# Context rows of a two-layer diffusion block: normalised rows written to memory and transposed behind four token tiles

## The chip, the cores and the metric

The kernel runs on one core of one Trainium2 chip. The metric is the device time of one execution in microseconds, the median of several runs. Each run is one launch of the whole program.

## The reference

Two layers work on 1024 latent tokens and 256 context tokens of width 1024. Layer 0 is grouped-query attention, layer 1 multi-head latent attention. Both begin in the same way, and layer 1 reads what layer 0 has made:

```python
h  = rms_norm(x, norm_w)   * (1.0 + scale[:, None, :]) + shift[:, None, :]
hc = rms_norm(ctx, norm_w) * (1.0 + scale_c) + shift_c
...
k, kr = split(h @ w_in ...)          # layer 1: 256 latent columns and 32 rotary columns
kv = rms_norm(kv_a, kv_a_norm) @ w_kv_b
k_nope, v = split(kv); k_rope = axial_rope(rms_norm(k_r, k_rope_norm))
...
x   = x + gate * y
ctx = ctx + gate_c * yc              # layer 0 only
```

Layer 1 needs the context for its keys and values alone, and only the latent stream is returned.

## The kernel before

Everything is float32. A product of two matrices is made of three products of TensorE (PE), of the high and low parts of both operands (`mm3`, lines 93 to 95); a high part is a cast on ScalarE (ACT), a low part a subtraction on VectorE (DVE) or, in turn, on GpSimd (POOL) (`sub_any`, line 136). Tokens come in ten tiles of 128 rows: tiles 0 to 7 are latent, 8 and 9 the context. DMAs are issued by SP, in the order of its queue; an issue that has to wait holds up those behind it.

Around the change the program has two stages.

The first is the output projection of layer 0 (`out_proj`, from line 710). For each tile in turn PE makes two products of 512 columns (`y`), DVE multiplies them by the gate (line 750), DVE and POOL add the residual (line 751), and `sink0` follows. `sink0` writes a latent tile to `x1d` in memory (line 1363), normalises its rows in place in the tile `xt` (`norm_rows`: the squares on ACT, line 256, their root on POOL, line 119, the scaling on DVE, line 258) and collects pairs of tiles. `flush` calls `modulate` for a pair, one tile later than it is complete: PE transposes the two tiles' rows in 16 pieces (line 270), DVE applies layer 1's scale and shift (line 274), ACT casts (line 278), and DVE or POOL subtracts. The result is `hh`, `hl`: the operand of layer 1's products, with tokens as columns. The last pair is the context; its `flush` stands behind the loop.

The second stage makes layer 1's keys and values. `staged` runs five steps over the ten tiles, each step some tiles behind the one before: `kv_compress` (24 products of 288 columns, then squares, roots and scaling to the row tile `kvn`, lines 1431 to 1440, and for the 32 rotary columns four small steps on POOL, lines 1447 to 1450), `kv_latent` (transposes of `kvn` by PE, lines 1457 and 1458, and their split `kvh`, `kvl`), `kv_expand` (24 products of 512 columns into `mmk` and `mmv`, the keys scaled by line 1470) and `kv_store` (line 1506 on). The products of `out_proj`, `kv_compress` and `kv_expand` share four PSUM buffers (`ps_mm`). At the beginning of this stage SP loads `w_kv_b` in four pieces of 512 KB, two pieces of the next weight, and small tables (line 1396: `bc_l1_kv_a_norm` and others; line 1401: `ropeB`). These tables lie in memory that the first stage's row tiles held. Three `wraw` buffers take the raw weights, so a piece is loaded only when an earlier one has been split.

A scheduler orders the instructions of both stages, but DVE keeps the order of the program text in the second.

Of the kernel before, what the change touches and what calls it, by code (L numbers as in the profile page):

```python
# [10 lines left out]
F32 = mybir.dt.float32  # L11
# [8 lines left out]
P = 128  # L20
D = 1024
KT = D // P
NL = 1024
NC = 256
NT = NL + NC
TL = NL // P
# [10 lines left out]
def hybrid_kernel(ctx: ExitStack, tc: tile.TileContext, ins: dict, out: bass.AP):  # L37
    nc = tc.nc
    pe, act, dve, pool, sp = nc.tensor, nc.scalar, nc.vector, nc.gpsimd, nc.sync
# [24 lines left out]
    x1d = dram.tile([NT, D], F32, name="x1d")  # L64
# [188 lines left out]
    def norm_rows(xt, small):  # L253
        junk = small.tile([P, D], BF16, name="junk", tag="junk", bufs=1)
        ss = small.tile([P, 1], F32, name="xss", tag="xss")
        act.activation(junk, xt, AF.Square, accum_out=ss)
        rs = rstd_of(small, ss, D, "x")
        dve.tensor_scalar(xt, xt, rs, None, op0=ALU.mult)

    def modulate(l, pair, xs, hT, ps_tp, tmpp, share=2, k2s=range(KT // 2)):  # L260

        cond = 1 if pair == 4 else 0
        hh, hl = hT[cond]
        cs = slice(0, 256) if cond else slice(pair * 256, pair * 256 + 256)
        for k2 in k2s:
            t = ps_tp.tile([P, 512], F32, name="tp", tag="tp")
            for kk in range(2):
                for j in range(2):
                    k = 2 * k2 + kk
                    pe.transpose(t[:, kk * 256 + j * P: kk * 256 + (j + 1) * P], xs[j][:, k * P:(k + 1) * P], ident)  # L270
            h = tmpp.tile([P, 512], F32, name="hmod", tag="w512")
            for kk in range(2):
                k = 2 * k2 + kk
                dve.tensor_scalar(h[:, kk * 256:(kk + 1) * 256], t[:, kk * 256:(kk + 1) * 256],
                                  A[l][:, k, cond:cond + 1], Bv[l][:, k, cond:cond + 1], op0=ALU.mult, op1=ALU.add)
            hv = h.rearrange("p (k n) -> p k n", k=2)
            hi = hh[:, 2 * k2:2 * k2 + 2, cs]
            act.copy(hi, hv)
            sub_any(hl[:, 2 * k2:2 * k2 + 2, cs], hv, raw(hi), share)
# [29 lines left out]
    class Attention:  # L309
# [382 lines left out]
        def flush(self):  # L692
            self.run_deferred(1 << 30)
# [94 lines left out]
    ps_tp = stT.enter_context(tc.tile_pool(name="pstp0", bufs=3, space=PSUM, reuse_waits="tile"))  # L788
# [554 lines left out]
    with ExitStack() as st:  # L1343
        xp = st.enter_context(tc.tile_pool(name="xpp0", bufs=4, **right))
        gp = st.enter_context(tc.tile_pool(name="gp0", bufs=1, **right))
        wk = st.enter_context(tc.tile_pool(name="wk1a", bufs=3, **right))
        small = st.enter_context(tc.tile_pool(name="sml1a", bufs=3, **right))
        pad(small, 224)
        stO = ExitStack()
        op = stO.enter_context(tc.tile_pool(name="opp0", bufs=3, **right))  # L1350
        hold = []
        hT1 = []

        def flush(upto):
            while len(hold) >= upto and hold:
                pair, xs = hold.pop(0)
                modulate(1, pair, xs, hT1, ps_tp, wk)

        xs_of = {}

        def sink0(tt, xt):
            if tt < TL:
                sp.dma_start(x1d[tt * P:(tt + 1) * P, :], xt)
            norm_rows(xt, small)
            xs_of.setdefault(tt // 2, []).append(xt)
            if tt % 2 == 0:
                flush(1)
            else:
                hold.append((tt // 2, xs_of[tt // 2]))

        def started0():
            at.flush()
            stL.close()
            hT1.append(alloc_hT(stl, "hlat1", NL))

        def resid0(tt):
            return x_in[tt * P:(tt + 1) * P, :] if tt < TL else ctx_in[(tt - TL) * P:(tt - TL + 1) * P, :]

        out_proj(0, wo, resid0, sink0, TT, op, xp, gp, ps_mm, first, started0, False)
        stO.close()  # L1380
        hT1.append(alloc_hT(stc, "hctx1", NC))
        flush(1)
    hT = hT1


# [2 lines left out]
    def proj1(tt, w, cols):  # L1388
        ps = ps_mm.tile([P, 512], F32, name="mm", tag="mm")
        lh, ll = h_cols(hT, tt)  # L1390
        mm3(ps[:, :cols], lh, ll, lambda k: w[0][:, k, :], lambda k: w[1][:, k, :], range(KT))
        return ps

    def bcast(tab, name, n):
        t = tab.tile([P, n], F32, name="bc_" + name)
        sp.dma_start(t, ins[name].rearrange("(o d) -> o d", o=1).broadcast_to([P, n]))
        return t
# [12 lines left out]
    with ExitStack() as st:  # L1410
# [4 lines left out]
        latp = st.enter_context(tc.tile_pool(name="latp1a", bufs=4, **right))  # L1415
        small = st.enter_context(tc.tile_pool(name="sml1b", bufs=3, **right))

        w_kva = bcast(tab, "l1_kv_a_norm", 256)
        w_kr = bcast(tab, "l1_k_rope_norm", 32)
        w_kn = tab.tile([P, 1], F32, name="w_kn")  # L1420
# [4 lines left out]
        wkv_v = [w.rearrange("p k (h c d) -> p k h c d", c=2, d=64) for w in wkvb]  # L1425

        def kv_compress(tt, _):
            ps = proj1(tt, wkvr, 288)
            ss = small.tile([P, 2], F32, name="kvss", tag="kvss")
            sq = wk.tile([P, 512], F32, name="sq", tag="w512")  # L1430
            act.activation(sq[:, :256], ps[:, :256], AF.Square, accum_out=ss[:, 0:1])
            act.activation(sq[:, 256:288], ps[:, 256:288], AF.Square, accum_out=ss[:, 1:2])
            ms = small.tile([P, 2], F32, name="kvms", tag="kvms")
            dve.tensor_scalar(ms[:, 0:1], ss[:, 0:1], 1.0 / 256, EPS, op0=ALU.mult, op1=ALU.add)
            dve.tensor_scalar(ms[:, 1:2], ss[:, 1:2], 1.0 / 32, EPS, op0=ALU.mult, op1=ALU.add)
            rs = small.tile([P, 2], F32, name="kvrs", tag="kvrs")
            pool.tensor_tensor(rs, ms, mhalf[:, :2], op=ALU.pow)
            kn = wk.tile([P, 512], F32, name="kvn", tag="w512")
            dve.scalar_tensor_tensor(kn[:, :256], ps[:, :256], rs[:, 0:1], w_kva, op0=ALU.mult, op1=ALU.mult)
            dve.scalar_tensor_tensor(kn[:, 256:288], ps[:, 256:288], rs[:, 1:2], w_kr, op0=ALU.mult, op1=ALU.mult)  # L1440
            if tt < TL:
                r_ = kn[:, 256:288]
                t2 = small.tile([P, 2, 2, 8], F32, name="krt2", tag="krt2")
                rv = r_.rearrange("p (a s d) -> p a s d", a=2, s=2)
                sv = sinB[:, tt, :].rearrange("p (a s d) -> p a s d", a=2, s=2)
                for s_ in range(2):
                    pool.tensor_mul(t2[:, :, s_, :], rv[:, :, 1 - s_, :], sv[:, :, s_, :])
                t3 = small.tile([P, 32], F32, name="krt3", tag="krt3")
                pool.tensor_mul(t3, r_, cosB[:, tt, :])
                pool.tensor_add(r_, t3, t2.rearrange("p a s d -> p (a s d)"))  # L1450
            return kn
# [349 lines left out]
```

## Time and profile before

| | us |
|---|---|
| median of 3 runs | 1704.43 (1702.04 to 1705.49) |
| the profiled execution's own time | 1703.22 |
| its span | 1701.4 |
| PE busy | 1663.7 |
| DVE busy | 1042.7 |
| ACT busy | 641.6 |
| POOL busy | 961.3 |

The span is the time from the first to the last instruction in the trace. The output projection of layer 0 ends at about 869 us of it, and the compression of layer 1 runs from there to about 952. Times in the trace are us from the start of the span; a row gives start, duration, engine, line and operation, what is written and read, and in brackets how long the engine sat idle before it and what ended that. Rows named SPq are DMA issues of SP.

### The profile page before, as it was taken

Reading aid. Unit: us, or ns where it says so; the run is one execution under the profiler, and the core shown is the slowest. Engines: PE = TensorE matmul, PEld = TensorE weight load, DVE = VectorE, ACT = ScalarE, POOL = GpSimd, SP = SyncE. Lnnn points to the kernel's source line nnn. Section 1 sums busy time; section 2 is a strip of 40 time slices with the busy share of each in tenths; the row PEclk is TensorE's granted clock in tenths of the full one; section 3 lists DMA queues with packets and bytes.
Section 4 is the critical chain, followed back from the end, with each engine's and each line's share of the span. In section 5 each row is a group of like instructions: output and inputs, shape, how many; then the busy total and the mean of one; then the engine's idle time right before and its main releaser. Section 6 shows DMA issues by size and latency. Waiting matters only on the chain. (4 is left out here: it accounts for less than half of the span.)

```text
span 1701.4 us, 27386 instructions
## 1 busy us (share of the span) xinstructions
PE 1663.7 (98%) x10212; PEld 1195.3 (70%) x10212; DVE 1042.7 (61%) x1807; ACT 641.6 (38%) x943; POOL 961.3 (57%) x646
## 2 busy tenths in 40 slices
PE   8999999999999999999989999999999999999998
PEld 5776768775555555557878889886766667667587
DVE  3765552357788777725575657754778777777231
ACT  4642222124455544432244543330434434344310
POOL 2773441218789988753235555350668787787521
PEclk9999999999999999999999999999999999999999
DMA  9557854521242422146433766776565555653451
GB/s 312 171 149 241 257 171 149 152 81 45 63 120 63 112 63 61 36 132 214 135 98 111 230 198 183 215 206 150 130 144 134 132 122 118 145 126 90 121 166 73
DMA packets 219821, 238.97 MB, mean 140 GB/s; under 512 B 23016, under 2 KB 159192, under 8 KB 219688
## 3 DMA queue, kind: packets, MB, share of 16 engines
q1 hardware_dynamic: 219264, 237.11, 49.5%
q8 instruction: 81, 1.33, 0.3%
q14 instruction: 52, 0.43, 0.1%
q10 hardware_dynamic: 424, 0.11, 0.0%
HBM read 163.37 MB, written 73.63 MB: 139 GB/s over the span
## 5 line engine op out<-in xcount | busy, mean ns | idle before, releaser
L395 DVE TENSOR_REDUCE m<-mx 128x1 f32<-128x512 f32 x512 | 336.0, 687 | 176.6 <-PE mx L393 171.6
L508 ACT ACTIVATE p<-st 128x1024 f32<-128x1024 f32 x328 | 335.9, 1027 | 170.9 <-PE st L501 137.5
L542 POOL TENSOR_TENSOR acp<-acp,p 128x1024 f32<-128x1024 f32 x128 | 305.4, 2386 | 7.8
L555 PE MATMUL av<-p,v 128*64 128x512 f32 x1312 | 289.9, 595 | 0.0
L555 PEld LDWEIGHTS av<-p,v 128*64 128x64 f32 x1312 | 90.9, 137 | 180.5 <-issue 177.9
L542 POOL TENSOR_TENSOR acp<-p 128x1024 f32<-128x1024 f32 x34 | 81.4, 2397 | 149.0 <-ACT p L508 148.9
L542 POOL TENSOR_TENSOR acp<-acp,acd 128x1024 f32<-128x1024 f32 x60 | 141.9, 2365 | 22.3 <-DVE acd L528 19.2
L528 DVE TENSOR_REDUCE acd<-p 128x512 f32<-128x1024 f32 x124 | 144.6, 1219 | 7.8 <-ACT p L508 7.8
L136 POOL TENSOR_TENSOR wb<-wraw,wa 128x512 fp32r<-128x512 f32 (+3 forms) x73 | 96.1, 1335 | 78.7 <-ACT wa L157 78.6
L93 PE MATMUL mm<-wa,hh 128*128 128x512 f32 (+2 forms) x336 | 127.2, 379 | 1.7 <-ACT hh L890 1.7
L501 PE MATMUL st<-QH,KH 64*128 64x512 f32 x320 | 122.9, 407 | 1.0 <-DVE gth L303 1.0
L95 PE MATMUL mm<-wa,hl 128*128 128x512 f32 (+2 forms) x336 | 121.3, 361 | 1.4 <-DVE hl L893 1.4
L94 PE MATMUL mm<-wb,hh 128*128 128x512 f32 (+2 forms) x336 | 120.9, 360 | 0.0
L501 PE MATMUL st<-QH,KL 64*128 64x512 f32 x320 | 119.6, 395 | 0.0
L501 PE MATMUL st<-QL,KH 64*128 64x512 f32 x320 | 118.9, 392 | 0.0
L576 ACT COPY os<-av 128x512 f32<-128x512 f32 x36 | 21.1, 587 | 255.9 <-PE av L555 214.5
L93 PE MATMUL y<-wa,oh 128*128 128x512 f32 (+1 forms) x296 | 114.3, 386 | 1.0 <-DVE yt L750 1.0
L95 PE MATMUL y<-wa,ol 128*128 128x512 f32 (+1 forms) x296 | 113.7, 384 | 0.0
L94 PE MATMUL y<-wb,oh 128*128 128x512 f32 (+1 forms) x296 | 113.7, 384 | 0.0
L404 DVE TENSOR_REDUCE m<-mx 128x2 f32<-128x512 f32 x144 | 95.4, 688 | 24.1 <-PE mx L403 19.0
L393 PE MATMUL mx<-KH,QH 64*128 64x512 f32 x256 | 102.6, 407 | 0.3 <-DVE m L404 0.3
L93 PE MATMUL mm<-hh,wa 128*128 128x512 f32 x256 | 102.1, 399 | 0.4 <-DVE qt L1675 0.4
(240 smaller groups left out, 4016.0 us busy)
## 6 DMA issues: line engine op xcount, KB each, us to landing
mraw<-in_l_w_mod SPq DMA_DIRECT2D x64, 256.0 KB
wraw<-in_l_w_in SPq DMA_DIRECT2D x28, 512.0 KB
KH<-k1h SPq DMA_DIRECT2D x32, 320.0 KB
KL<-k1l SPq DMA_DIRECT2D x32, 320.0 KB
rb<-rrow SPq DMA_DIRECT2D x72, 128.0 KB
mraw<-in_l_w_mod SPq DMA_DIRECT2D x16, 512.0 KB
sgd<-gth SPq DMA_DIRECT2D x32, 256.0 KB
wraw<-in_l_w_out SPq DMA_DIRECT2D x16, 512.0 KB
```

Source lines behind the costliest of these rows:

```text
L93: pe.matmul(ps, lhsT=lh(k), rhs=rh(k), start=first and i == 0, stop=False)
L94: pe.matmul(ps, lhsT=lh(k), rhs=rl(k), start=False, stop=False)
L95: pe.matmul(ps, lhsT=ll(k), rhs=rh(k), start=False, stop=last and i == len(ks) - 1)
L136: eng.tensor_sub(lo, a, b)
L393: pe.matmul(held["m"][:, cs], lhsT=q[:, t * P:(t + 1) * P], rhs=k[:, ks], start=j == 0, stop=j == len(pairs) - 1)
L395: dve.reduce_max(s["m"][:, i, n:n + 1], held["m"], axis=AX.X)
L404: dve.reduce_max(s["m"][:, 2 * i:2 * i + 2, 2 if u["kind"] == "lat" else 0], m.rearrange("p (a b) -> p a b", a=2), axis=AX.X)
L501: pe.matmul(ps[:, n * 512:(n + 1) * 512], lhsT=lh, rhs=rh, start=j == 0, stop=j == last)
L508: act.activation(p, ps, AF.Exp, scale=self.ops["scale"])
L528: dve.reduce_sum(t[:, ns], p2.rearrange("p a n -> p n a")[:, ns, :], axis=AX.X)
L542: pool.tensor_add(t, a, b)
L555: pe.matmul(s["av"][64 * n:64 * n + 64, :], lhsT=s["v"][:, kt, u["vc"]:u["vc"] + 64], rhs=p[:, n * 512:(n + 1) * 512], start=kt == kts[0], ...
```

## The change

The context's two tiles are treated apart. `sink0` still normalises their rows, but then writes them to rows 1024 to 1279 of `x1d`, which nothing used before, and returns; the pair of tiles 6 and 7 is flushed at tile 8 as it was. The `flush` behind the loop is gone. In the second stage two new row tiles (pool `xc1`, 4 KB a partition each) are loaded from these rows of `x1d`; the loads stand ahead of the small tables in the text. `kv_compress` of tile 4 first calls `modulate` for the context, with these tiles and with its own working tiles.

```diff
@@ sink0 @@
             norm_rows(xt, small)
+            if tt >= TL:
+                sp.dma_start(x1d[tt * P:(tt + 1) * P, :], xt)
+                if tt == TL:
+                    flush(1)
+                return
             xs_of.setdefault(tt // 2, []).append(xt)
@@ behind out_proj @@
         hT1.append(alloc_hT(stc, "hctx1", NC))
-        flush(1)
@@ layer 1, keys and values @@
+        xc = st.enter_context(tc.tile_pool(name="xc1", bufs=2, **right))
+        ctx_rows = [xc.tile([P, D], F32, name="xt", tag="xt") for _ in range(2)]
+        for j, xt in enumerate(ctx_rows):
+            sp.dma_start(xt, x1d[NL + j * P:NL + (j + 1) * P, :])
         w_kva = bcast(tab, "l1_kv_a_norm", 256)
@@ kv_compress @@
         def kv_compress(tt, _):
+            if tt == 4:
+                modulate(1, 4, ctx_rows, hT, ps_tp, wk)
             ps = proj1(tt, wkvr, 288)
```

In the changed kernel the lines of the second stage are numbered higher by 4 (up to the tables) and by 10 (from `kv_compress` on); the stores of the context are line 1366, its loads line 1425. Numbers behind tile names tell one buffer of a name from another.

PE, at the first transposes of the context that need tile 9. Before, `xt_8347` and `xt_8461` are tiles 8 and 9, and `mm_8701` is tile 1's compression:

```order
L94 MATMUL mm_8701<-wb_8615,hh_7649 128x288
L95 MATMUL mm_8701<-wa_8614,hl_7650 128x288
L270 MATMUL tp_8537<-ident_70,xt_8461 128x128 [waits DVE_49]
L270 MATMUL tp_8537<-ident_70,xt_8347 128x128
L270 MATMUL tp_8537<-ident_70,xt_8461 128x128
L270 MATMUL tp_8547<-ident_70,xt_8461 128x128
```

Now no context transpose stands there. PE goes through the 96 products of tiles 0 to 3; the rows below are the end of them, where `mm_8784` is tile 3's, `mm_8881` tile 4's, and `kvn_8661`, `kvn_8704` are the latent rows of tiles 0 and 1:

```order
L94 MATMUL mm_8784<-wb_8584,hh_7649 128x288
L95 MATMUL mm_8784<-wa_8583,hl_7650 128x288
L1467 MATMUL tp_8713<-ident_70,kvn_8661 128x128 [waits DVE_49]
L1467 MATMUL tp_8713<-ident_70,kvn_8661 128x128
L93 MATMUL mm_8881<-wa_8583,hh_7649 128x288 [waits DVE_49,PE_49]
L94 MATMUL mm_8881<-wb_8584,hh_7649 128x288
L95 MATMUL mm_8881<-wa_8583,hl_7650 128x288
L1468 MATMUL tp_8713<-ident_70,kvn_8661 32x128 [waits Pool_49]
L93 MATMUL mm_8881<-wa_8583,hh_7649 128x288
L94 MATMUL mm_8881<-wb_8584,hh_7649 128x288
L1467 MATMUL tp_8770<-ident_70,kvn_8704 128x128 [waits DVE_49]
```

The sixteen context transposes moved behind tile 2's latent transposes, around the last products of tile 4's compression and the first of tile 0's expansion.

SP, from the last pieces of weights to the tables of the second stage. Before:

```order
L153 DMA wraw_8652<-in_l1_w_kv_b 128x1024 [waits DMAHW4_49,DMAHW1_49,DVE_49]
L153 DMA wraw_10011<-in_l1_w_in 128x2x384 [waits DMAHW5_49,DMAHW2_49,DVE_49]
L153 DMA wraw_10017<-in_l1_w_in 128x2x384 [waits DMAHW3_49,DVE_49]
L1396 DMA bc_l1_q_a_norm_8584<-in_l1_q_a_norm 128x384 [waits DMAHW7_49,PE_49]
L1396 DMA bc_l1_q_norm_8586<-in_l1_q_norm 128x96 [waits DMAHW0_49]
L1401 DMA ropeB_8588<-in_rope1 128x512
L1396 DMA bc_l1_kv_a_norm_8607<-in_l1_kv_a_norm 128x256
```

Now, where `xt_8462` is tile 9 and `xt_8572`, `xt_8573` are the tiles read back:

```order
L1425 DMA xt_8572<-x1d_79 128x1024 [waits DMAHW5_49,DMAHW1_49,PE_49]
L153 DMA wraw_8621<-in_l1_w_kv_b 128x1024 [waits DMAHW2_49,DVE_49]
L153 DMA wraw_10021<-in_l1_w_in 128x2x384 [waits DMAHW7_49,DMAHW3_49,DVE_49]
L1366 DMA x1d_79<-xt_8462 128x1024 [waits DMAHW0_49,DVE_49]
L153 DMA wraw_10027<-in_l1_w_in 128x2x384 [waits DMAHW4_49,DVE_49]
L153 DMA wraw_10033<-in_l1_w_in 128x2x384 [waits DMAHW6_49,DVE_49]
L1400 DMA bc_l1_q_a_norm_8546<-in_l1_q_a_norm 128x384 [waits DMAHW0_49]
L1400 DMA bc_l1_q_norm_8548<-in_l1_q_norm 128x96
L1405 DMA ropeB_8550<-in_rope1 128x512 [waits DMAHW5_49]
L1425 DMA xt_8573<-x1d_79 128x1024
L1400 DMA bc_l1_kv_a_norm_8576<-in_l1_kv_a_norm 128x256 [waits DMAHW7_49]
```

Two stores and two loads of 512 KB are new in this queue, and a third piece of the next weight comes ahead of the tables. DMAs take the eight semaphores DMAHW0 to DMAHW7 in turn: the store of tile 9 has DMAHW0, for which `bc_l1_q_a_norm` waits; before, it waited for PE.

DVE, where the context is scaled. Before, between tile 9's normalisation and tile 0's first row of `kv_compress`:

```order
L258 TENSOR_SCALAR xt_8461<-xt_8461,x_rs_8528 128x1024
L136 TENSOR_TENSOR wb_8639<-wraw_8648,wa_8638 128x1024
L274 TENSOR_SCALAR hmod_8542<-tp_8537,A1_102,B1_104 128x256 x2
L274 TENSOR_SCALAR hmod_8552<-tp_8547,A1_102,B1_104 128x256 x2
L274 TENSOR_SCALAR hmod_8562<-tp_8557,A1_102,B1_104 128x256 x2
L136 TENSOR_TENSOR hl_8536<-hmod_8552,hh_8535 128x512
L274 TENSOR_SCALAR hmod_8572<-tp_8567,A1_102,B1_104 128x256 x2
L136 TENSOR_TENSOR wb_8639<-wraw_8652,wa_8638 128x1024
L136 TENSOR_TENSOR hl_8536<-hmod_8572,hh_8535 128x512
L1434 TENSOR_SCALAR kvms_8687<-kvss_8683 128x1
```

Now, between the split of tile 2's latent (`krl_8836`) and `kv_compress` of tile 4 (`kvms_8910`):

```order
L87 TENSOR_TENSOR krl_8836<-tp_8827,krh_8835 32x128
L274 TENSOR_SCALAR hmod_8846<-tp_8841,A1_102,B1_104 128x256 x2
L274 TENSOR_SCALAR hmod_8856<-tp_8851,A1_102,B1_104 128x256 x2
L136 TENSOR_TENSOR hl_8538<-hmod_8856,hh_8537 128x512
L274 TENSOR_SCALAR hmod_8866<-tp_8861,A1_102,B1_104 128x256 x2
L274 TENSOR_SCALAR hmod_8876<-tp_8871,A1_102,B1_104 128x256 x2
L136 TENSOR_TENSOR hl_8538<-hmod_8876,hh_8537 128x512
L1444 TENSOR_SCALAR kvms_8910<-kvss_8906 128x1
```

The same ten operations of DVE, with their casts on ACT, moved as a block past the first four tiles of the loop; the split of `w_kv_b`'s last piece now follows the third's at once.

## The prediction

> **What bounds the kernel now.** The page gives TensorE (PE) 98% of the span; so I look for the few microseconds in which PE has nothing to run near the lines that the diff touches. PE's waits between 840 and 1000 us come first (waiter, releaser: total, times, longest), then the busy times by 20 us (PE, PEld, DVE, ACT, POOL; at the end PE's granted clock, the DMA engines' share and GB/s).
>
> ```profile
> PE 1663.7 (98%) x10212; PEld 1195.3 (70%) x10212; DVE 1042.7 (61%) x1807; ACT 641.6 (38%) x943; POOL 961.3 (57%) x646
> ...
> PE tp L270 <- DVE xt L258: 5.2, 1, 5.2
> ...
> 860.00:880.00 20.00, 14.76 (x82) 12.85 (x81) 15.43 (x20) 9.50 (x18) 9.29 (x9) 0.93 0.35 115
> 880.00:900.00 20.00, 19.13 (x122) 17.74 (x122) 13.27 (x40) 9.11 (x34) 10.06 (x26) 0.89 0.32 89
> ```
>
> One wait of 5.2 us stands there: the context's transposes (L270) wait for tile 9's normalised rows (L258). It is followed by a dip of the granted clock to 0.89. The timeline of PE around it:
>
> ```profile
> 869.33 0.60 PE L270 MATMUL tp<-ident,xt 128*128 128x128 f32 x4
> ...
> 879.51 2.82 PE L270 MATMUL tp<-ident,xt 128*128 128x128 f32 x12 [5.24 <-DVE xt L258]
> ...
> 882.61 0.44 PE L95 MATMUL mm<-wa,hl 128*128 128x288 f32 x1
> 882.85 0.44 PE L93 MATMUL mm<-wa,hh 128*128 128x288 f32 x1
> ...
> 886.76 0.29 PE L94 MATMUL mm<-wb,hh 128*128 128x288 f32 x1
> 886.90 0.29 PE L95 MATMUL mm<-wa,hl 128*128 128x288 f32 x1
> ```
>
> After the idle stretch the compression's products come every 0.24 us (882.61 to 882.85), later every 0.13 to 0.14 (886.76 to 886.90).
>
> What PE waited for, on ScalarE (ACT), DVE and GpSimd (POOL):
>
> ```profile
> 875.60 1.04 ACT L157 CAST wa<-wraw 128x1024 fp32r<-128x1024 f32 x1 [0.96 <-DMA wraw<-in_l_w_kv_b]
> 876.55 1.05 ACT L256 ACTIVATE junk<-xt 128x1024 bf16<-128x1024 f32 x1
> 877.83 0.15 DVE L117 TENSOR_SCALAR x_ms<-xss 128x1 f32<-128x1 f32 x1
> 878.70 0.75 DVE L258 TENSOR_SCALAR xt<-xt,x_rs 128x1024 f32<-128x1024 f32 x1 [0.73 <-POOL x_rs L119]
> 879.47 1.05 ACT L157 CAST wa<-wraw 128x1024 fp32r<-128x1024 f32 x1 [0.84 <-DMA wraw<-in_l_w_kv_b]
> ...
> 886.94 0.14 DVE L1434 TENSOR_SCALAR kvms<-kvss 128x1 f32<-128x1 f32 x1
> ```
>
> The squares of tile 9's rows (876.55) stand behind a cast of w_kv_b that waits for its load; tile 9 is ready at 879.45. The change touches nothing of this, so 879.45 holds after it too. The last two rows serve below.
>
> **PE's bill before.** Full-speed durations, from the next two tiles of the same loop:
>
> ```profile
> 897.36 0.48 PE L93 MATMUL mmk<-wa,kvh 128*128 128x512 f32 x1
> ...
> 902.92 0.29 PE L93 MATMUL mm<-wa,hh 128*128 128x288 f32 x1
> ...
> 906.07 0.38 PE L1457 MATMUL tp<-ident,kvn 128*128 128x128 f32 x2
> ...
> 906.32 0.48 PE L93 MATMUL mmk<-wa,kvh 128*128 128x512 f32 x1
> ...
> 907.79 0.39 PE L93 MATMUL mmv<-wa,kvh 128*128 128x512 f32 x1
> ...
> 856.68 1.91 PE L270 MATMUL tp<-ident,xt 128*128 128x128 f32 x16
> 858.35 0.48 PE L93 MATMUL y<-wa,oh 128*128 128x512 f32 x1
> ```
>
> A tile's compression is 906.07 - 902.92 = 3.15 us, its latent transposes 0.25, its expansion 902.92 - 897.36 = 5.56, the first key product of the next 1.47, sixteen L270 transposes 1.67. From 869.33 to 907.79 (first value product of tile 1) PE does six compressions (18.9), five latent transposes (1.25), 5.56 + 1.47 and 1.67: 28.85 us. The stretch lasts 38.46, so 9.6 us are lost: 5.24 of wait, about 2.6 of half clock (12 transposes in 2.82 instead of 1.25; nine products at 0.24 instead of 0.13), the rest in small waits.
>
> **The change part by part.** The transposes leave the place of the wait, and PE goes on with four compressions. What is due at their end is tile 0's normalised latent kvn, since transposing it is PE's next step. The orders of PE above show it: behind the last product of tile 3 (mm_8784) comes the transpose of kvn_8661, which waits for DVE.
>
> PE gets there at 869.35 + 4 x 3.15 = 881.95, without a wait on the way. The next compression needs tile 0's PSUM buffer, which kvn frees as well: nothing is left to fill with.
>
> When is kvn there? Before, these rows (DVE, POOL, and the SP queue's own):
>
> ```profile
> 887.98 0.48 DVE L1439 SCALAR_TENSOR_TENSOR kvn<-mm,kvrs,bc_l_kv_a_norm 128x256 f32<-128x256 f32 x1 [0.83 <-POOL kvrs L1437]
> 890.01 0.48 DVE L1439 SCALAR_TENSOR_TENSOR kvn<-mm,kvrs,bc_l_kv_a_norm 128x256 f32<-128x256 f32 x1 [1.26 <-POOL kvrs L1437]
> ...
> 889.94 0.25 POOL L1450 TENSOR_TENSOR kvn<-krt,krt 128x32 f32<-128x32 f32 x1
> ...
> 891.42 0.25 POOL L1450 TENSOR_TENSOR kvn<-krt,krt 128x32 f32<-128x32 f32 x1
> ...
> 877.93 3.06 SPq L153 DMA_DIRECT2D wraw<-in_l_w_in  x2
> 882.36 0.34 SPq L1396 DMA_DIRECT2D bc_l_q_a_norm<-in_l_q_a_norm  x1
> ...
> 883.70 0.43 SPq L1396 DMA_DIRECT2D bc_l_kv_a_norm<-in_l_kv_a_norm  x1
> ...
> SPq L1396 <- PE tp L270: 1.3, 1, 1.3
> ```
>
> kvn multiplies by bc_l_kv_a_norm, which SP loads only here: the tables lie where layer 0's row tiles lay, so they waited for the last L270 (1.3 us, until 882.36).
>
> In SP's order after the change, shown above, the first table load waits for DMAHW0: the landing of tile 9's store, which reads the memory it overwrites. Behind it in SP's queue stand the other tables, the 512 KB re-read of tile 9, and then bc_l1_kv_a_norm. The price of such a store, from two earlier ones and the L258 that each held up:
>
> ```profile
> 823.95 0.33 SPq L1363 DMA_DIRECT2D x1d<-xt  x1
> ...
> 826.82 0.76 DVE L258 TENSOR_SCALAR xt<-xt,x_rs 128x1024 f32<-128x1024 f32 x1 [1.42 <-DMA x1d<-xt]
> ...
> 846.72 0.33 SPq L726 DMA_DIRECT2D gb<-gated  x1
> 847.48 0.33 SPq L1363 DMA_DIRECT2D x1d<-xt  x1
> ...
> 852.46 1.60 DVE L258 TENSOR_SCALAR xt<-xt,x_rs 128x1024 f32<-128x1024 f32 x1 [0.33 <-DMA x1d<-xt]
> ```
>
> Alone it lands 2.87 us after its issue, behind another 512 KB issued 0.76 earlier 4.98 after. Tile 9's store goes out at 879.5, 1.6 us after a load of w_in; I take 3.6, nearer to the lone one: 883.1. Issues follow each other by about 0.47 (882.36 to 883.70 in three steps, 0.45 each), so bc_l1_kv_a_norm goes out four issues later, at 885.0. It is small, but has a 512 KB load just ahead and two w_in loads and tables before that; 4.98 is its nearest row, so kvn starts at **890.0**. Bounds: not before 884.3 (store alone, landing at once), and 891.5 if the store too takes 4.98. kvn's other input is earlier. Tile 0's squares follow the last w_kv_b cast directly now, which ended at 880.52 and may slip by 0.5; with about 0.9 for the squares, 0.4 for DVE to finish that piece's split and the 1.04 from 886.94 to 887.98 the factor is there by 883.4.
>
> The sum of PE's losses now:
> - the first wait, 890.0 + 0.5 - 881.95 = 8.5 us. After the wait of 5.24 the products ran at half pace, so they will after this one. But half pace falls on the seven products and few transposes among the next waits, which end when POOL ends, so it is charged nothing; bounds 0 and, if it outlasts them by the compression of tile 4 (3.15 at half pace, half of that lost), 1.5. The Trainium skill, "TensorE: Matmul & The Clock Gate", section "HAM oscillation — how this bites in real kernels", puts PE back to half clock after some 3.4 us of idling and lets it stay there as long as idle gaps go on; by that rule the upper bound holds, and the sum below would be 7.6 instead of 6.1.
> - the rotary part on POOL. Before it ended 889.94 + 0.25 - 887.98 = 2.2 us after kvn, and tile 1's 3.7 after (891.42); PE then had compressions to fill with. Now it waits 1.2, 0.65, and for tile 2, whose chain stands behind these, 0.6 and 0.75: 3.2.
> - the eight scalings and two subtractions of the context now stand in DVE's row between tiles 2 and 4 of the loop. Their price is in the groups:
>
> ```profile
> L274 DVE TENSOR_SCALAR hmod<-tp,A,B x40: 528/535/543, 786.7 to 884.4; 128x256 f32<-128x256 f32 x40
> L136 DVE TENSOR_TENSOR hl<-hmod,hh x10: 678/694/1629, 790.2 to 886.3; 128x512 fp32r<-128x512 f32 x10
> ...
> 901.14 1.64 POOL L119 TENSOR_TENSOR kn_rs<-kn_ms,mhalf 128x8 f32<-128x8 f32 x1 [0.79 <-DVE kn_ms L117]
> ```
>
> 8 x 0.535 + 2 x 0.69 = 5.7 us of DVE ahead of tile 4's kvn and tile 0's key scaling, which frees PE's PSUM and has POOL's 1.64 us roots (kn_rs) in its chain. Followed through the orders, PE waits 0.95 before tile 5's compression, 0.7 at tile 4's rotary part, 1.8 and 0.55 for the two scalings: 4.0. Bounds 0 (DVE catches up) and 5.7.
>
> The two stores, two reads and the 8 KB buffer are otherwise free. Tile 8's store goes out near 862.6 and has landed long before it is read; its 512 KB delays w_kv_b's last quarter by perhaps 0.5, whose cover is the expansion, over 15 us later. If that cover were gone it would cost that 0.5.
>
> 8.5 + 3.2 + 4.0 = 15.7 lost instead of 9.6: **+6.1 us**. Afterwards PE runs without waiting as before and the shift stays. The profiled execution took 1703.22 us (span 1701.4), so it would take 1709.3; it lay 1.2 under the median of 1704.43, to which I add: **1710.5**.
>
> **The rivals.** 0.2%, about what a measurement here can tell from no change, is 3.4 us.
> - *The tables are not late (no change).* If transfers overlap so that bc_l1_kv_a_norm, a quarter of the lone store's size, lands 2.0 us after its issue (under that store's 2.87), kvn starts at 887.0: 3.0 less, +3.1, **1707.5**. For it: the DMA engines' share is only 0.32 to 0.35 in the windows quoted first. Against it: the 4.98 us row. The Trainium skill, "DMA: Bandwidth & Descriptors", section "Anatomy of one DMA — SWDGE (gpsimd) path", fits 2.0 us plus bytes over 436 KB/us: an estimate of 2.3 us for this 128 KB load, 3.2 for the store (the lone store's 2.87 is near it), and the sum would be this rival's.
> - *The new wait is short (faster).* Place: the first L1467. If the table landed at 884.3, and DVE's context work were hidden in PE's 5.56 us expansions, the loss is 15.7 - 5.7 - 4.0 = 6.0: -3.6, **1700.8**. Either alone doesn't suffice; it decides only with kvn before about 884.5.
> - *The context's work on DVE is not caught up.* All 5.7 instead of 4.0, kvn at 891.5 and 1.3 of half clock: 1.7 + 1.5 + 1.3 more, +10.6, some 1715. The stretch 880 to 900 has DVE 66% busy, which leaves room to recover.
> - *The change is not what it says.* PE's order shows all sixteen transposes behind the compressions; only PE waiting for the re-read at L270 could undo it, and the re-read is issued ahead of the table on which PE already waits.
>
> **How the numbers follow.** Slower by over 0.2%: 0.70, the forecast and the third rival. Within 0.2%: 0.25, the first rival, or kvn near 889 with DVE's work hidden. Faster: 0.05. The likeliest case's own range is 1707 to 1714. For eight in ten it has to reach down into no change, to 1703.5 (kvn at 887 and DVE's 4.0 hidden: -0.9), and up to 1714.
>
> **What would show it.** Right: no L270 wait near 875; one PE wait of 7 to 10 us at about 882 for DVE's kvn, that row released by DMA bc_l_kv_a_norm; the first table issue at 882.5 to 884.5; short waits on POOL kvn and DVE kn by 912. Wrong: kvn starting before 888 or released by POOL kvrs, or PE at tile 1's first value product before 911.

## The result, and the profile after

| | before | after |
|---|---|---|
| median of 14 runs each | 1706.42 (1702.04 to 1709.86) | 1711.85 (1708.87 to 1716.51) |
| the profiled execution's own time | 1703.22 | 1716.51 |
| its span | 1701.4 | 1714.6 |

The changed kernel takes 1.0033 times as long, with an interval of 1.0025 to 1.0042: about 5.5 us more.

The two profiled executions are 13.3 us apart, and not all of that belongs to the change: the changed kernel's trace is the longest of its 14 runs. In it PE starts the output projection 3.6 us later (754.48 instead of 750.90), ahead of the first line that the change touches. From its first product there to the start of its last it takes 120.7 us, where before took 118.2. Up to that point the change adds only tile 8's store, and experiments 2 and 4 below, which have that store too, took 117.9 and 117.6. From the last `y` product on, where the rest of the change works, the profiled pair differs by 7.2 us at PE's last instruction (834.8 us after that product against 827.6). So the traces are compared from that product on. First PE's waits after the change (waiter, releaser: total, times, longest), between 840 and 1010 us:

```profile
PE tp L1467 <- DVE kvn L1449: 10.1, 1, 10.1
PE tp L1516 <- DVE kn L1480: 2.7, 2, 1.9
PE mmv L93 <- DVE kn L1480: 1.5, 1, 1.5
PE tp L1468 <- POOL kvn L1460: 0.9, 3, 0.4
PE mm L93 <- ACT v L1502: 0.7, 1, 0.7
```

The wait of 5.2 us at L270 is gone, and one of 10.1 us stands at L1467, the transposes of tile 0's normalised latent. The second row stood there before with the same numbers. The timeline of PE:

```profile
875.18 0.39 PE L95 MATMUL y<-wa,ol 128*128 128x512 f32 x1
875.40 0.29 PE L93 MATMUL mm<-wa,hh 128*128 128x288 f32 x1
...
887.91 0.30 PE L95 MATMUL mm<-wa,hl 128*128 128x288 f32 x1
898.33 0.69 PE L1467 MATMUL tp<-ident,kvn 128*128 128x128 f32 x2 [10.13 <-DVE kvn L1449]
...
903.29 0.44 PE L94 MATMUL mm<-wb,hh 128*128 128x288 f32 x1
903.53 0.40 PE L95 MATMUL mm<-wa,hl 128*128 128x288 f32 x1
903.76 0.30 PE L93 MATMUL mm<-wa,hh 128*128 128x288 f32 x1
903.90 0.29 PE L94 MATMUL mm<-wb,hh 128*128 128x288 f32 x1
...
921.42 0.47 PE L93 MATMUL mmv<-wa,kvh 128*128 128x512 f32 x1 [1.51 <-DVE kn L1480]
```

PE does 96 products without a stop, then stands still from 888.2 to 898.3. The products after it come every 0.24 us until 903.53, then every 0.14. The stretch of the prediction, from 875.40 to the first value product of tile 1 at 921.42, lasts 46.02 us where it lasted 38.46: 7.6 more.

Why kvn was late stands in the rows of DVE, POOL and SP:

```profile
885.77 0.75 DVE L258 TENSOR_SCALAR xt<-xt,x_rs 128x1024 f32<-128x1024 f32 x1 [0.73 <-POOL x_rs L119]
...
888.29 1.23 DVE L136 TENSOR_TENSOR wb<-wraw,wa 128x1024 fp32r<-128x1024 f32 x1 [0.64 <-ACT wa L157]
...
897.79 0.48 DVE L1449 SCALAR_TENSOR_TENSOR kvn<-mm,kvrs,bc_l_kv_a_norm 128x256 f32<-128x256 f32 x1 [8.14 <-DMA bc_l_kv_a_norm<-in_l_kv_a_norm]
...
889.72 0.70 POOL L1447 TENSOR_TENSOR kvrs<-kvms,mhalf 128x2 f32<-128x2 f32 x1 [3.99 <-DVE kvms L1445]
```

```profile
886.55 0.33 SPq L1366 DMA_DIRECT2D x1d<-xt  x1
887.68 2.24 SPq L153 DMA_DIRECT2D wraw<-in_l_w_in  x2
889.98 0.46 SPq L1400 DMA_DIRECT2D bc_l_q_a_norm<-in_l_q_a_norm  x1
...
891.43 0.43 SPq L1425 DMA_DIRECT2D xt<-x1d  x1
891.90 0.43 SPq L1400 DMA_DIRECT2D bc_l_kv_a_norm<-in_l_kv_a_norm  x1
```

DVE waits 8.1 us, and from 890.42 on, when POOL has kvn's other input kvrs done, it waits 7.4 us for bc_l_kv_a_norm alone. SP issues that load 5.35 us after tile 9's store (886.55), behind two loads of w_in, three of the other tables and the re-read. The windows (PE, PEld, DVE, ACT, POOL busy, PE's granted clock, the DMA engines' share, GB/s) show what else happens then:

```profile
886.00:890.00 4.00, 2.20 (x17) 1.97 (x15) 3.01 (x5) 2.68 (x13) 0.28 (x1) 1.00 0.93 274
890.00:892.00 2.00, 0.00 (x0) 0.00 (x0) 0.00 (x0) 0.00 (x0) 0.43 (x1) 1.00 0.85 237
892.00:894.00 2.00, 0.00 (x0) 0.00 (x0) 0.00 (x0) 0.00 (x0) 0.00 (x0) 0.88 1.02 230
894.00:896.00 2.00, 0.00 (x0) 0.00 (x0) 0.00 (x0) 0.00 (x0) 0.00 (x0) 0.50 0.88 332
896.00:898.00 2.00, 0.00 (x0) 0.00 (x0) 0.21 (x1) 0.00 (x0) 0.00 (x0) 0.50 0.37 107
898.00:900.00 2.00, 1.41 (x5) 1.06 (x5) 0.74 (x5) 0.00 (x0) 1.49 (x5) 0.50 0.00 0
...
900.00:920.00 20.00, 18.56 (x104) 15.94 (x104) 11.82 (x36) 8.86 (x30) 9.21 (x22) 0.91 0.11 34
```

From 890.4 to 897.8 none of the five engines does anything, while the DMA engines are busy for 0.85 to 1.02 of the time until 896. PE's granted clock holds after its last product (888.2) and then falls to 0.50; a mean of 0.88 from 892 to 894 puts the fall at about 893.5. The clock is still at 0.50 when PE has work again. The 0.91 of the last window is worth 3.6 us at half clock, so until about 903.6, which agrees with the pace of the products.

### The profile page after: what moved, and what is told of

Its sections match the earlier page's. It is cut to its first block, busy times and chain, and to the rows that moved or that the text cites. A ratio compares the mean times of both kernels' runs of the same rounds, so it can differ in the third digit from the quotient of the medians.

```text
span 1714.6 us, 27388 instructions
## 1 busy us (share of the span) xinstructions
PE 1668.7 (97%) x10212; PEld 1197.2 (70%) x10212; DVE 1043.2 (61%) x1807; ACT 640.8 (37%) x943; POOL 959.8 (56%) x646
## 4 chain that ended last, share of the span: by engine, by line
PE 82%; DMA 4%; POOL 4%; DVE 4%; issue 3%; ACT 1%; SPq 1%; ACTq 0%; DVEq 0%; POOLq 0%
PE st L501 20%; PE av L555 15%; PE mm L93 8%; PE mm L95 7%; PE mm L94 7%; PE mx L393 6%; PE y L93 3%; PE y L94 3%; PE y L95 3%; PE mx L403 1%; PE mx L597 1%; PE pm L200 1%; POOL acp L542 1%; DMA xt<-in_x 1%; PE tp L998 1%
## 5 line engine op out<-in xcount | busy, mean ns | idle before, releaser
L95 PE MATMUL mm<-wa,hl 128*128 128x512 f32 (+2 forms) x336 | 122.4, 364 | 1.6 <-DVE hl L893 1.6
L501 PE MATMUL st<-QH,KH 64*128 64x512 f32 x320 | 122.2, 404 | 1.0 <-DVE gth L303 1.0
L94 PE MATMUL mm<-wb,hh 128*128 128x512 f32 (+2 forms) x336 | 122.2, 364 | 0.0
L501 PE MATMUL st<-QH,KL 64*128 64x512 f32 x320 | 119.0, 392 | 0.0
```

The source lines that it names most:

```text
L94: pe.matmul(ps, lhsT=lh(k), rhs=rl(k), start=False, stop=False)
L95: pe.matmul(ps, lhsT=ll(k), rhs=rh(k), start=False, stop=last and i == len(ks) - 1)
L501: pe.matmul(ps[:, n * 512:(n + 1) * 512], lhsT=lh, rhs=rh, start=j == 0, stop=j == last)
```

## The experiments

Three theories for the lost time were put to the test.

- **A**, the prediction's: bc_l_kv_a_norm is loaded late, because the tables lie in memory that tile 9's store still reads and because the store and the re-read stand ahead of it in SP's queue.
- **B**: the 2 MB that the context now moves (two stores and two reads of 512 KB) cost the time by their traffic.
- **C**: the context's ten operations on DVE, now in the middle of the loop, cost it.

All kernels at a glance, each timed on one chip beside the kernel before. "Output" is the time from the first `y` product to the start of the last, "keys, values" from there to the first product of 384 columns, which is the next stage; both from the profiled execution. "First wait" is the longest of PE's waits in the second. The rows of each experiment carry the line numbers of its own kernel.

| kernel | ratio to before | output, us | first wait, us | keys, values, us |
|---|---|---|---|---|
| before | 1 | 118.2 | 5.2 | 112.0 |
| after | 1.0033 (1.0025 to 1.0042) | 120.7 | 10.1 | 120.0 |
| 1 tables early | 1.0022 (1.0009 to 1.0035) | 122.5 | 4.5 | 113.1 |
| 2 re-reads last | 1.0037 (1.0024 to 1.0050) | 117.9 | 8.2 | 118.2 |
| 3 rows stay in SBUF | 1.0037 (1.0024 to 1.0051) | 120.9 | 6.7 | 112.0 |
| 4 context at tile 7 | 1.0033 (1.0021 to 1.0045) | 117.6 | 9.8 | 118.1 |
| 5 before, tables early | 1.0016 (1.0003 to 1.0029) | 122.2 | 5.6 | 113.4 |
| 6 tables at tile 4 | 1.0000 (0.9988 to 1.0011) | 119.2 | 3.8 | 112.2 |
| 7 as 6, casts later | 1.0056 (1.0042 to 1.0069) | 121.8 | 4.4 | 121.8 |
| 8 before, casts later | 1.0031 (1.0020 to 1.0042) | 117.8 | 5.4 | 119.0 |
| 9 tables in own memory | 1.0009 (0.9999 to 1.0019) | 120.4 | 4.3 | 112.9 |
| 10 as 6, ACT in order | 1.0061 (1.0046 to 1.0077) | 119.8 | 5.3 | 122.4 |
| 11 before, ACT in order | 1.0010 (0.9998 to 1.0021) | 117.8 | 3.2 | 113.5 |
| 12 tables behind tile 4's store | 1.0000 (0.9986 to 1.0013) | 117.8 | 4.7 | 112.5 |

**1. Layer 1's tables early.** All small tables get memory of their own (5 KB a partition) and are loaded where layer 0's output products begin.

```diff
@@ started0 @@
+            tb = stl.enter_context(tc.tile_pool(name="tabE", bufs=1, reuse_waits="tile"))
+            early.update(w_qa=bcast(tb, "l1_q_a_norm", 384), w_q=bcast(tb, "l1_q_norm", 96), rope=rope_tables(tb),
+                         w_kva=bcast(tb, "l1_kv_a_norm", 256), w_kr=bcast(tb, "l1_k_rope_norm", 32),
+                         w_kn=tb.tile([P, 1], F32, name="w_kn"))
```

> The changed kernel, with the small tables (norm weights and rotary tables of layer 1) loaded into memory of their own at the start of layer 0's output projection; stores, reads and transposes of the context stay as changed. Theory A (the norm weight's load, held up by tile 9's store and the re-read, makes PE wait 10.1 us): kvn of tile 0 no longer starts on a DMA but on its root on POOL, the first PE wait falls from 10.1 to 3 to 4 us, and the time is 5 to 8 us under the changed kernel's, -3 to +1 against before. Theory B (the 2 MB of context traffic itself delays the weights and PE): wait stays above 7 us, +3 to +6 against before. Theory C (the context's ten DVE operations in the middle of the loop are the cost): first wait gone but the time falls by no more than 2, +3.5 or more against before.

Measured 1708.94, ratio 1.0022. Two waits of its profile, one from each of the two stages:

```profile
PE y L93 <- DVE yt L750: 3.9, 1, 3.9
```

```profile
PE tp L1469 <- DVE kvn L1451: 5.1, 2, 4.5
```

The first wait falls from 10.1 to 4.5, and the stage of keys and values is 1.0 us longer than before instead of 8.0, although all of the context's traffic and DVE work is still there. But a wait of 3.9 us is new in the output products, and it gives back much of that: A forecast at most 1 us over before, and the ratio is worth 3.8 us. So A holds for the stage, and the edit has a price of its own.

**2. Re-reads behind the tables.** In the text the two loads of the context move behind the tables; tile 9's then stands behind them in SP's queue.

```diff
-        for j, xt in enumerate(ctx_rows):
-            sp.dma_start(xt, x1d[NL + j * P:NL + (j + 1) * P, :])
         w_kva = bcast(tab, "l1_kv_a_norm", 256)
...
+        for j, xt in enumerate(ctx_rows):
+            sp.dma_start(xt, x1d[NL + j * P:NL + (j + 1) * P, :])
```

> The changed kernel, with the two re-reads of the context behind the small tables in the program text; SP then issues the re-read of tile 9 after them, still behind tile 9's store. Theory A: the norm weight's load goes out 0.45 us earlier and without 512 KB just ahead of it; kvn of tile 0 starts about 2 us earlier, the first wait is about 8 instead of 10.1 us, the time 2 us under the changed kernel's (+3.5 against before). Theories B and C: no difference to the changed kernel (+5.5).

Measured 1712.17, ratio 1.0037; the load and its user, from SP's and DVE's timelines:

```profile
888.48 0.43 SPq L1400 DMA_DIRECT2D bc_l_kv_a_norm<-in_l_kv_a_norm  x1
```

```profile
893.30 0.48 DVE L1449 SCALAR_TENSOR_TENSOR kvn<-mm,kvrs,bc_l_kv_a_norm 128x256 f32<-128x256 f32 x1 [6.61 <-DMA bc_l_kv_a_norm<-in_l_kv_a_norm]
```

Without the 512 KB ahead of it the small load takes 4.8 us from issue to use instead of 5.9, and the first wait is 8.2. The re-read ahead of the table is thus worth 1.9 us of the wait; what holds the rest, this run doesn't tell apart. In the whole time the 1.9 us don't show: A forecast 3.5 us over before, and the ratio is worth 6.3.

**3. Rows stay in SBUF.** Line 258 writes tiles 8 and 9 into two row tiles of their own, which the second stage reads; nothing is stored or read back. To make room, layer 0's output products have two `yt` buffers where they had three, so this kernel changes that stage too. The cut below leaves out the line of `yt`, the two tiles' allocation and the loads that go.

```diff
@@ sink0 @@
-            norm_rows(xt, small)
+            norm_rows(xt, small, ctx_rows[tt - TL] if tt >= TL else None)
             if tt >= TL:
-                sp.dma_start(x1d[tt * P:(tt + 1) * P, :], xt)
```

> The transposes stand behind four token tiles as changed, but the normalised context rows are written to two tiles that stay in SBUF: no store, no re-read (one of layer 0's small product buffers is halved to two to make room). The tables then wait for tile 9's normalisation only. Theory A: the norm weight is issued near 881 on the scale of the trace before and lands near 885, the first wait is 4 to 6 us, the time -2 to +2 against before. Theory B: the same or better, -4 to 0, with the first wait under 4. Theory C: +3 or more, since the DVE operations stay where they are.

Measured 1710.87, ratio 1.0037. From its DVE timeline:

```profile
888.46 0.48 DVE L1447 SCALAR_TENSOR_TENSOR kvn<-mm,kvrs,bc_l_kv_a_norm 128x256 f32<-128x256 f32 x1 [3.45 <-DMA bc_l_kv_a_norm<-in_l_kv_a_norm]
```

Even without any store the table is late: its load now waits for line 258, which frees tile 9's memory, and goes out at 884.01. In this profile, the fastest of the kernel's six runs, the stage of keys and values is as long as before's, and 2.7 us are lost in the output products, where PE waits 3.6 us at L270 for tile rows. Whether the missing `yt` buffer does that wasn't tried, and the rest of this kernel's loss stays open. As a test of B it doesn't count.

**4. The context at tile 7.** `modulate` is called three tiles later (`if tt == 7`).

> The changed kernel, with the context's transposes and scaling at tile 7 of the loop instead of tile 4. Theory A: the first wait stays near 10 us; the waits for DVE's key scaling and ACT's value copy behind it (1.5 and 0.7 us) vanish, so the time is 1 to 2.5 us under the changed kernel's, +3 to +4.5 against before. Theory C: 4 us or more under the changed kernel's. Theory B: as the changed kernel.

Measured 1709.03, ratio 1.0033. From PE's waits:

```profile
PE tp L1467 <- DVE kvn L1449: 9.8, 1, 9.8
...
PE tp L270 <- DVE tl L1521: 1.3, 1, 1.3
```

The first wait is nearly the changed kernel's 10.1. The waits of 1.5 us for kn and 0.7 us for v behind it are gone (0.3 us for v is left), and one of 1.3 us for DVE's tl is new. By the ratio the time is that of the changed kernel, where A forecast 1 to 2.5 us less and C 4 us less or more. So the place of the context in the loop changes little; that speaks against C.

**5. The kernel before, with the tables early.** The edit of experiment 1 on the kernel before.

> The kernel before, with layer 1's small tables loaded early, at the start of layer 0's output products, into memory of their own, as in the first experiment. That experiment's profile showed PE waiting 3.9 us for DVE's yt at 782.65, in the output products, where the kernel before waits 1.0 in all. If the early loads are what makes that wait, this kernel shows it too (3 us or more near 780) and takes 1707 to 1709. If the wait was a matter of that one execution, this kernel takes what the kernel before takes, 1704 to 1706, with a wait of 1 us there.

Measured 1710.12, ratio 1.0016, and PE waits 3.5 us for yt. So by the ratio the early loads cost 2.7 us (1.6 thousandths of 1706.7) by themselves, with an interval of 0.5 to 5. Taken from experiment 1's 1.0022 it leaves 0.6 thousandths, 1 us, for the whole change; the two intervals overlap, so this 1 us is not shown.

**6. Tables at tile 4.** The same loads, written behind tile 4's store.

> The changed kernel with the same tables in memory of their own, loaded behind tile 4's store, when layer 0's output products are half done. Theory A (the late norm weights are nearly the whole loss): the wait for kvn of tile 0 is 5 us or less, none over 1.5 us in the output products, 1704 to 1707, within 0.1% of before. Theory B (the 2 MB of context traffic) and theory C (the context's DVE work in the loop): 1709 to 1712 still. If the first experiment's 1708.9 came from anything but the early loads: again 1708 to 1710.

Measured 1706.84 against 1706.72, ratio 1.0000: the loss is gone, with the whole change in place. So A carries, and neither B nor C is the cause of the loss. This doesn't make the context's traffic and scaling free, since the change also takes away before's wait of 5.2 us. In its place stands a first wait of 3.8 us with half clock behind it (granted 0.50 from 888 to 892), and the stage comes out as long as before's. One point of the expectation failed: PE waits 2.4 us for yt. The scheduler had not kept five of the seven loads at tile 4; they go out between 748.8 and 751.3, as they do in experiment 9. What is left of the first wait, 3.8 us, has its root on ACT:

```profile
883.84 1.04 ACT L157 CAST wa<-wraw 128x1024 fp32r<-128x1024 f32 x1 [1.52 <-DMA wraw<-in_l_w_kv_b]
884.79 0.38 ACT L1448 ACTIVATE sq<-mm 128x256 f32<-128x256 f32 x1
```

Tile 0's squares, whose products PE had done by 876.3, stand behind the last cast of w_kv_b, which waits for its load. The next two and experiments 10 and 11 try to take that away.

**7. and 8. The split of w_kv_b later**, on top of 6 and on the kernel before.

```diff
+        kvb = []
-        wkvb = load_weight(ins["l1_w_kv_b"], 2, 0, 2048, 1)
+        wkvb = load_weight(ins["l1_w_kv_b"], 2, 0, 2048, 1, None, kvb)
@@ kv_compress @@
+            if tt == 1:
+                for piece in kvb:
+                    piece()()
```

> As the kernel before it in this list, and layer 1's kv_b weights are split behind the second tile's squares in the program, which puts one of ACT's four casts behind the squares of tiles 0 to 2. What is left of the first wait (4.5 us with early tables) is put down to these casts, which wait for the weights' DMA: then the wait falls by one cast and its landing, 2 to 3 us, to about 2, and the kernel takes 1702 to 1705. If the wait hangs on something else (the squares' own order, the clock), it stays at 4 to 5 and the time is the other kernel's within 1 us; if the values' products then wait for the last cast, it is slower than that one by 2 to 4.

> The kernel before with the same later split of the kv_b weights alone. Its largest wait, 5.2 us for tile 9's rows, stands behind two of the four casts, which do not move: if that wait is what counts, 1704 to 1706, no change. If the last cast is on the path (the squares of tile 0 stand behind it in the kernel before), up to 2 us less, 1702 to 1704; if the last kv_b piece then comes too late for the first key and value products, 2 to 4 us more.

Measured 1716.18 (1.0056) and 1711.45 (1.0031): both worse. The fourth piece of w_kv_b is loaded with its split, and so it came late: issued at 891.97 and 892.46, where experiment 6 issued it at 879.38 and the kernel before at 875.93. The edit undid itself, and says nothing of the casts.

**9. Tables in their own memory, loaded where the change loads them.** Only the pool differs.

```diff
-    w_qa = bcast(qtab, "l1_q_a_norm", 384)
-    w_q = bcast(qtab, "l1_q_norm", 96)
-    cosB, sinB = rope_tables(qtab)
+    w_qa = bcast(tabE[0], "l1_q_a_norm", 384)
+    w_q = bcast(tabE[0], "l1_q_norm", 96)
+    cosB, sinB = rope_tables(tabE[0])
...
-        w_kva = bcast(tab, "l1_kv_a_norm", 256)
+        w_kva = bcast(tabE[0], "l1_kv_a_norm", 256)
```

> The changed kernel with the tables' loads where they are in the program, but into memory of their own, so that no load has to wait for tile 9's store; the order of the instructions then puts these loads far ahead of the weights. Theory A in its narrower form (the reuse of tile 9's memory makes the load late): the wait for kvn of tile 0 falls from 10.1 to 5 us or less and the kernel takes what before takes, 1704.5 to 1708, ratio at most 1.0012, unless the loads meet the weights' loads in layer 0's output products, as in the first experiment: then a wait of 2 us or more for yt and 1707 to 1709. If the reuse of the memory is not the cause: 1710 to 1713 still.

Measured 1707.42, ratio 1.0009. The wait for kvn:

```profile
PE tp L1469 <- DVE kvn L1451: 4.9, 2, 4.3
```

The first wait is 4.3, so the memory that the tables share with the row tiles is what made them late: without it the scheduler puts the loads far ahead. To leave the memory shared and move only the w_in loads, which stand ahead of the tables in the changed kernel's queue, was not tried. The scheduler puts the tables here, in SP's queue:

```profile
746.35 0.59 SPq L611 DMA_DIRECT2D sg<-sgd  x1
747.04 0.53 SPq L1402 DMA_DIRECT2D bc_l_q_a_norm<-in_l_q_a_norm  x1
...
749.51 0.43 SPq L1402 DMA_DIRECT2D bc_l_k_rope_norm<-in_l_k_rope_norm  x1
751.54 1.11 SPq L613 DMA_DIRECT2D rb<-rrow  x2
752.75 0.53 SPq L726 DMA_DIRECT2D gb<-gated  x1
```

Five small loads stand between the last loads of layer 0's attention (sg and rb). Before, rb goes out 2.7 us after this sg (746.73 to 749.42), here 5.2; in experiment 6, which has the same order, 4.8. PE then waits 2.7 us for yt near 774.

**10. and 11. ACT in the program's order**, with the split of w_kv_b written behind tile 1's squares, three of its four loads left where they were; on top of 6 and on the kernel before.

```diff
+        landed = [piece() for piece in kvb[:3]]
@@ kv_compress @@
+            if tt == 1:
+                for parts in landed:
+                    parts()
+                kvb[3]()()
...
-        with in_order(mybir.EngineType.DVE):
+        with in_order(mybir.EngineType.DVE), in_order(mybir.EngineType.Activation):
```

> The changed kernel with the tables loaded behind tile 4's store, and ACT's work of the loop in the program's order, with the kv_b split written behind tile 1's squares: tile 9's squares and those of tiles 0 and 1 then stand ahead of all four casts. What is left of the first wait (3.8 us with the tables at tile 4) is put down to the casts, which wait for the weights' DMA: then that wait is under 1 us, the key products start 3 to 4 us sooner after the start of the compression, and the kernel takes 1701 to 1704, less than before. If the transposes' rows then wait behind the casts on ACT instead, or the fixed order costs elsewhere in the loop: 1706 to 1712.

> The kernel before with the same order of ACT alone. Its 5.2 us wait for tile 9's rows is put down to tile 9's squares, which stand behind two casts: then the wait is under 1 us and the kernel takes 1700 to 1704. If the fixed order costs as much elsewhere in the loop, 1705 to 1711. Against the kernel above it says what the change is worth once the casts are out of the way: nothing (within 1 us) by theory A, since its extra work has no other price.

Measured 1714.66 (1.0061) and 1708.74 (1.0010). In the second the wait for tile 9's rows falls from 5.2 to 1.8, where under 1 was expected, and PE's timeline has a new one for POOL:

```profile
875.00 1.53 PE L270 MATMUL tp<-ident,xt 128*128 128x128 f32 x12 [1.83 <-DVE xt L258]
...
889.10 0.28 PE L1464 MATMUL tp<-ident,kvn 128*32 128x128 f32 x1 [3.17 <-POOL kvn L1456]
```

In the first, SP's queue shows a trap like the one that made the change slow:

```profile
877.42 0.33 SPq L1379 DMA_DIRECT2D x1d<-xt  x1
883.15 0.32 SPq L1436 DMA_DIRECT2D xt<-x1d  x1
887.10 0.33 SPq L153 DMA_DIRECT2D wraw<-in_l_w_kv_b  x1
```

The last piece of w_kv_b stands behind tile 9's store and re-read now. The re-read goes out 5.7 us after the store, whose rows it reads, and the weights at 887.10; ACT waits 9.2 us for them with tile 0's latent queued behind. Whether the 4 us that are left of the first wait can be won with the casts out of the way stays open.

**12. Tables held behind tile 4's store.** Experiment 6 with SP's order fixed at this place.

```diff
             if tt == 4:
-                tables()
+                with in_order(mybir.EngineType.SP):
+                    sp.dma_start(x1d[tt * P:(tt + 1) * P, :], xt)
+                    tables()
```

> The changed kernel with the tables in memory of their own and their loads held behind tile 4's store in SP's queue. In the two kernels whose tables had memory of their own, five of the seven loads were issued between 747 and 752, inside the end of layer 0's attention, and PE then waited 2.4 to 2.7 us for yt near 774. If those early issues made that wait, it is 1.0 us or less here; the wait for kvn of tile 0 stays at about 4; and the kernel takes 1702.5 to 1705.5, ratio 0.998 to 1.000, before or a little under it. If the wait for yt has another cause, it stays over 2 us and the time is that of the two kernels, 1.0000 to 1.0009.

Measured 1704.96 against 1706.85, ratio 1.0000 (0.9986 to 1.0013). SP's queue and PE's wait in the output products:

```profile
812.75 1.40 SPq L1375 DMA_DIRECT2D x1d<-xt  x1
814.19 0.42 SPq L1338 DMA_DIRECT2D bc_l_q_a_norm<-in_l_q_a_norm  x1
...
816.18 0.46 SPq L1338 DMA_DIRECT2D bc_l_kv_a_norm<-in_l_kv_a_norm  x1
```

```profile
PE y L93 <- DVE yt L750: 0.2, 1, 0.2
```

The wait for yt is gone with the early issues, and the output products take 117.8 us again. The link holds over all traces: in the six kernels with five tables issued among the last loads of the attention (1, 5, 6, 7, 9 and 10) PE waits 2.2 to 3.9 us for yt, in the other eight 1.0 at most. How the later loads hold up yt was not followed. In the whole time this kernel can't be told from experiment 6. The changed kernel then stands level with the one before. It isn't shown to beat it, and no kernel here did.

## Why the prediction was right

The direction, the place and the cause came out as forecast, and the sum was near. Part of that nearness is luck: its terms were not all of the right size, and one step gave its number for another reason than the one that it names. The stretch starts 6.07 us later in this trace (875.40 instead of 869.33), which is taken off below.

| step | forecast | measured |
|---|---|---|
| PE reaches L1467 | 881.95 | 888.20 - 6.07 = 882.1 |
| tile 9's rows ready | 879.45 | 886.52 - 6.07 = 880.5 |
| tile 9's store issued | 879.5 | 880.5 |
| first table issued | 883.1 | 883.9 |
| bc_l1_kv_a_norm issued | 885.0 | 885.8 |
| kvn starts | 890.0 | 891.7 |
| first wait | 8.5 | 10.1 |
| waits for POOL's rotary part | 3.2 | 0.9 |
| waits by the context's work on DVE | 4.0 | 2.2 |
| half clock after the wait | 0, at most 1.5 | 2.5 |
| lost in all | 15.7 | 9.6 + 7.6 = 17.2 |

Two values lie outside the bounds that the prediction gave for them: kvn at 891.7 (at most 891.5) and half clock at 2.5 (at most 1.5). The sum came out near all the same, because the waits on POOL and DVE were shorter than forecast.

**Tile 9's rows**: "the change touches nothing of this, so 879.45 holds" failed by 1.0 us. The second cast of w_kv_b, ahead of tile 9's squares on ACT, started at 882.67 - 6.07 = 876.6 instead of 875.60. In experiment 3, without tile 8's store, it was 876.1, so the store ahead of these loads may hold half of it.

**From the store to the first table** it took 3.43 us, forecast 3.6, but what held it is not what the step named. The trace shows the two w_in loads in that time; the second waits for the raw buffer that DVE's split frees at 888.29 + 1.23 = 889.52, and the tables follow it at once. The landing of the store leaves no wait of its own, so it is luck that 3.43 is so near 3.6. The shared memory worked all the same, through the order: the table loads stand behind the store, and in experiment 9, where they have memory of their own, they go out 140 us earlier.

**The small load** took 5.9 us from issue to use, where the nearest row gave 5.0. The first rival had 2.0, with the fit of the Trainium skill's "DMA: Bandwidth & Descriptors" ("Anatomy of one DMA — SWDGE (gpsimd) path") beside it, an estimate of 2.3. The page gives that fit for DMAs issued by GpSimd, and these loads are issued by SP. The traces show 5.9 here, 4.8 in experiment 2 and 4.45 in experiment 3 (884.01 to 888.46), with the DMA engines' mean share at 0.79, 0.88 and 0.66 over these times. That decided against the rival.

**Half clock** was charged nothing, on the ground that half pace would fall on waits that end with POOL. It does, but it also goes on beyond them: from 898.33 to 903.76 PE runs at half pace but for 0.3 us, which costs 2.5. That half pace would end with the small waits was the part of the step that was wrong. It may also explain why the rotary waits are 0.9 instead of 3.2: slower products fill them, and the two terms are then partly the same microseconds. No run tells them apart.

The rule of the Trainium skill that the prediction cites ("TensorE: Matmul & The Clock Gate", "HAM oscillation — how this bites in real kernels") has PE back at half clock after an idle gap of some 3.4 us. The trace agrees for the gap of 10.1 us (granted 0.50 from about 893.5). In the 5.4 us at half pace PE was idle for only 0.3, so it was hardly idle gaps that kept it there, as the prediction reads that rule. Its sum by the rule was 7.6, and the stretch lost 7.6; the terms of the two differ, and that they meet is luck.

**The context's work on DVE** cost at most 0.7 before tile 5's compression, a wait that ended with ACT's copy of the values, and 1.5 at the second scaling: 2.2 instead of 4.0. Both waits are gone in experiment 4, where this work comes three tiles later. In experiment 6, with the work in the same place and the tables early, the value products don't wait for kn either. So it seems to be the price of a loop that is late already; no run measures it by itself.

About 1.4 us of the 17.2 are in gaps that no wait names. Tile 1's first value product came at 921.42 - 6.07 = 915.35, where a time before 911 was named as a refutation; the wait for kn, which was to come by 912, ended only then.

The runs' ratio puts the change at 5.5 us, the forecast had 6.1, the two traces 7.2 at the end. Experiments 2 and 4, with first waits of 8.2 and 9.8, have ratios of 1.0037 and 1.0033, and their stages of keys and values are 6.1 and 6.0 us longer than before's. So the changed kernel's own trace, with 8.0, is probably somewhat above its typical run there as well.

Of the rivals, *tables not late* fell with the 8.1 us row, *the new wait is short* with the 10.1 us. *Not caught up* came true in two of its three terms (kvn at 891.7 and 2.5 of half clock, where it had 891.5 and 1.3), but DVE's work cost 2.2 and not 5.7, and its +10.6 was not reached. *The change is not what it says* fell: the sixteen transposes start at 904.77, behind the four compressions.

## What to carry to other kernels

When a load of a few KB is read at the head of a stage, look where its memory was before and what stands ahead of it in its queue: here a 1 KB row of weights, spread to 128 KB, held PE for some 6 of the 10 us that it waited, and giving the row memory of its own and a quiet place in the queue took the loss away. A load that is moved forward has to be placed, not only freed, since seven small loads issued early cost 2.7 us in a stage that doesn't read them. And when an edit puts a store and its re-read into an in-order queue, look at the price for what stands behind them.

## What was not expected of the hardware

A load of 128 KB took 4.45 to 5.9 us from its issue to its first use while the DMA engines' mean share was 0.66 to 0.88, as much as the 512 KB stores quoted in the prediction (2.9 to 5.0) or more.

PE's granted clock stayed at 1.00 for some 5.3 us after its last product, fell to 0.50, and stayed there for another 5.3 us after PE had work again (898.33 to about 903.6); a wait of 10.1 us thus cost 12.6. The time until the fall is not fixed: worked out in the same way from the windows' means, it was 3.1 us in the kernel before (0.85 from 876 to 878, last product done at 874.27) and some 3.8 in experiment 2 (0.86 from 888 to 890, last product done at 885.69).
